# T4 of the value weights added on VectorE from raw buffers on chip; four raw buffers and 67 slots; the stores of x by column, head fetches and the parts of S2 moved

## The chip, the cores and the metric

The kernel runs on one core of one Trainium2 chip. The metric is device time in microseconds (us), lower is better. The engines are named as in the profile: PE is TensorE (PEld its weight loads), DVE VectorE, ACT ScalarE, POOL GpSimd, SP SyncE, which here issues transfers only. POOL issues transfers too, and those that add into their destination all go through it.

## The reference

Two decoder layers over 512 positions of width 2048, in float32. Each layer makes one wide projection of x, splits its columns among three groups of heads, multiplies each group's output by a gate, projects the result and normalises it with the residual.

```python
for l in range(DEPTH):                                  # DEPTH = 2
    h = einsum('bsd,dn->bsn', x, w_in[l])               # 2048 -> 8278 columns
    # 6 heads with a forget bias, 6 heads that see only their 128 best keys (16 index heads
    # score them), 4 heads into 256 memory tokens; each group's output times silu(gate)
    y = concatenate([y_fox, y_dsa, y_mem], axis=-1)
    y = einsum('bsn,nd->bsd', y, w_out[l])
    x = layer_norm(ALPHA * x + y, ln_gain[l], ln_bias[l])
```

## The kernel before

**Products.** Every float32 operand is split into a high part (`whi`, made by ACT) and the rest (`wlo`, made by DVE), and a product is three matmuls: high by high, high by low, low by high (lines 220 to 222). Weights come in chunks of 128 rows by 2048 columns (1 MB, tile `raw`). A chunk is used in two halves of 128 by 1024; each half is split by `split_w` three halves ahead of its matmuls, and `load_w` issues a chunk's load on SP two chunks ahead. There are three `raw` buffers and four `whi`/`wlo` pairs.

**Stages of a layer.** Projection of the memory tokens (`mv`, `mk`), the index heads and their scores (`small`, `iq`, `ix`), memory heads (`mq`, `mg`), **values** (kind `vs`: values, gates and some queries and keys), **heads** (`fq`, `fk`, `dq`, `dk`, each followed by its attention `attend`), and the output projection (`out`). The values and the output use a Strassen-like scheme: seven products, named P1, P7, Q6, Q4, Q5, P2 and Q3, replace eight, and take sums of weight blocks on the right (T1 to T4) and sums of x on the left (S1 to S4).

**The right sides T2 and T4 of the values.** Their chunks are not loaded but "grown". When the P7 chunk has been split, its `raw` buffer is kept, a transfer issued by POOL adds a block of the weights into it, and it becomes Q6's chunk; after Q6 another such transfer adds the (1, 0) block, and it becomes Q4's chunk. `grow_w` (lines 245 to 250) issues them: 32 transfers of 1 MB, 16 for Q6 and 16 for Q4, over two layers and four pairs of column groups. P2's chunk, used between them, is the same (1, 0) block, loaded from the same place in HBM.

**Order.** The program's order is written by hand (a manual schedule): each engine runs its instructions in that order. Side work is written as generators, advanced by `tick`: once in each half chunk, except that attention advances once a chunk while values or output run. `attend` issues, at its start, the fetches of the head's gates and values (`load_head`, line 882, on SP), and two ticks later it begins the transposes. `val_operands` makes S1 to S4 and splits them; `next_x` (line 933) ends a layer: it normalises the residual tiles `z`, transposes them into the next x (`xh`, `xl`), and then stores the 16 `z` tiles to HBM (`x1`, line 956). At the start of the second layer `residual_rows` (line 960) fetches those tiles, applies gain and bias (lines 968 and 969) and stores them again (line 970).

**Slots.** Everything of 128 by 512 float32 lives in one pool of 71 slots (`slot`). A new tile takes a slot that an earlier tile has left, and its first writer waits until the last reader of the earlier tile is done. The pool hands out slots that came free lately, so the distance between the two is often short. SP and POOL issue transfers in order: one that waits for its slot holds all later ones of its engine back.

The lines that the steps below touch: 213 and 214 (`split`), 241 (a chunk's load), 249 (the growing transfer), 466 (first writer of the memory heads' probabilities `pm`), 767 (sums of x), 777, 845 to 863 (values out of PSUM), 882, 968 to 970.

Of the kernel before, what the change touches and what calls it, by code (L numbers as in the profile page):

```python
# [14 lines left out]
ALU = mybir.AluOpType  # L15
AX = mybir.AxisListType

P = 128
# [68 lines left out]
VAL_OPENS = ("P1", "P7", "P2", "Q5")  # L87
VAL_ENDS = ("P1", "Q4", "P2", "Q3")
GROWN = {"Q6": ("P7", (0, 0)), "Q4": ("Q6", (1, 0))}


def layer_chunks(l):
# [80 lines left out]
def kernel(  # L173
# [12 lines left out]
):  # L186
    nc = tc.nc
    consts = ctx.enter_context(tc.tile_pool(name="consts", bufs=1))
    raws = ctx.enter_context(tc.tile_pool(name="raws", bufs=3))
    whl = ctx.enter_context(tc.tile_pool(name="whl", bufs=4))  # L190
    slots = ctx.enter_context(tc.tile_pool(name="slots", bufs=71))
    tiny = ctx.enter_context(tc.tile_pool(name="tiny", bufs=3))
    psum = ctx.enter_context(tc.tile_pool(name="psum", bufs=8, space=bass.MemoryType.PSUM))
    dram = ctx.enter_context(tc.tile_pool(name="dram", bufs=1, space=bass.MemoryType.DRAM))
# [30 lines left out]
    chunks = stream()  # L225
    raw, parts = {}, {}
    sums = {}
    grows = {}
    place = {c[:4]: i for i, c in enumerate(chunks)}
    for i, (kind, l, j, g, (how, key)) in enumerate(chunks):  # L230
        if how == "grown":
            grows[place[kind, l, (key[0], j[1]), g]] = i

    def load_w(i, pieces=1):
        if i < len(chunks) and chunks[i][4][0] != "grown":
# [8 lines left out]

    def grow_w(i):

        if i in grows:
            n = grows[i]
            nc.gpsimd.dma_start(raw[n], wall[chunks[n][4][1][1]], accum_op=ALU.add,
                                max_dma_last_dim=4 * DM)  # L250

    def last_half(i):

# [2 lines left out]
    def split_w(n, pieces=1, between=None):  # L256
        i, h = divmod(n, 2)
        if i < len(chunks):
            if last_half(i) and n < 2 * len(chunks) - 3:
                parts[n] = []  # L260
                for c in range(2):
                    hi, lo = slot("wh", F32R), slot("wl", F32R)
                    split(raw[i][:, h * 1024 + c * 512:h * 1024 + (c + 1) * 512], hi, lo)
                    parts[n].append((hi, lo))
                return
            hi = whl.tile([P, DM // 2], F32R, tag="whi", name=uid("whi"))
            lo = whl.tile([P, DM // 2], F32R, tag="wlo", name=uid("wlo"))
            w = DM // 2 // pieces
            for c in range(pieces):
                r = slice(c * w, (c + 1) * w)  # L270
                split(raw[i][:, h * 1024 + c * w:h * 1024 + (c + 1) * w], hi[:, r], lo[:, r])
                if between and c == 0:
                    between()
            parts[n] = (hi, lo)
            if last_half(i):
                parts[n] = [(hi[:, c:c + 512], lo[:, c:c + 512]) for c in (0, 512)]
            if h:
                t = raw.pop(i)
                if i in grows:
                    raw[grows[i]] = t  # L280


    mem_raw = {}
# [355 lines left out]
    def attend(l, kind, h):  # L639
# [15 lines left out]
        for qb in (3, 1, 0, 2):  # L655
            b, off, w = PACK[qb]
            c = slice(off, off + w)
# [12 lines left out]
                                     scale=rec[:, qb:qb + 1])  # L670

        before.append(probabilities)
        n = HEADS.index(key)
        load_head(("g", key), GATES + n // 4, n % 4)
        load_head(("v", key), VALUES + n // 4, n % 4)
        yield 2
        tp = [bank("pt") for _ in range(3)]
        for kt in range(4):
            tb, toff = PT_PACK[kt]
# [99 lines left out]
    def val_operands():  # L779
        add, sub = ALU.add, ALU.subtract  # L780
        a11, a12, a21, a22 = (0, 0), (0, 1), (1, 0), (1, 1)

        for i in range(4):
            val_sum("S3", i, ((a11, 0, add), (a21, 0, sub), (a11, 1, add), (a21, 1, sub)))
            yield 1
        for i in range(4):
            val_hi("S3", i)
            val_sum("S2", i, (("S3", 0, add), (a22, 0, add), (a22, 1, add)))
            yield 1
            val_lo("S3", i)  # L790
            yield 1
        for i in range(4):
            hi, lo = vleft["S2", i] = slot("vxh", F32R), slot("vxl", F32R)
            nc.scalar.activation(hi, vx["S2", i], AF.Copy, scale=-1.0)
            yield 1
            nc.vector.scalar_tensor_tensor(lo, vx["S2", i], -1.0, hi.bitcast(F32),
                                           op0=ALU.mult, op1=ALU.subtract)
        yield from wait_for("P7")
        making.append("S1")
        for n in range(9):  # L800
            if n < 4:
                val_sum("S1", n, ((a11, 0, add), ("S2", 0, sub), (a11, 1, add)))
            elif n < 8:
                val_sum("S4", n - 4, ((a12, 0, add), ("S2", 0, sub), (a12, 1, add)),
                        vx.pop(("S2", n - 4)))
            yield 1
            if n == 4:
                yield from wait_for("Q6")
            if n:
                name, i = (("S1", n - 1), ("S4", n - 5))[n > 4]  # L810
                val_lo(name, i)
            if n < 8:
                val_hi(*(("S1", n), ("S4", n - 4))[n > 3])
            yield 1
        making.clear()
# [95 lines left out]
    def norm_stats(st):  # L911
        mv, rs = small("mv", 2, bufs=4), small("rs", 1, bufs=4)
        nc.vector.bn_aggr(mv, stats.pop(st).rearrange("p (a b) -> p a b", a=8))
        nc.vector.tensor_scalar(rs, mv[:, 1:2], LN_EPS, None, op0=ALU.add)
        nc.gpsimd.tensor_tensor(rs, rs, mhalf, op=ALU.pow)
        return mv, rs
# [15 lines left out]

    def next_x():

        ms = [norm_stats(st) for st in range(4)]
        for c in range(4):
            for st in range(4):
                normalise(st, c, *ms[st])
            yield 1
        for k in range(KT):  # L940
            c, o = divmod(k, 4)
            tp = bank("xt")
            for st in range(4):
                nc.tensor.transpose(tp[:, st * P:(st + 1) * P], z[st, c][:, o * P:(o + 1) * P], ident)
            xf, hi, lo = slot("xf"), slot("xh", F32R), slot("xl", F32R)
            nc.scalar.activation(xf, tp, AF.Identity, bias=gcol[:, 1, k:k + 1],
                                 scale=gcol[:, 0, k:k + 1])
            nc.scalar.activation(hi, xf, AF.Copy)
            eng = nc.gpsimd if k % 2 else nc.vector
            eng.tensor_tensor(lo, xf, hi.bitcast(F32), op=ALU.subtract)  # L950
            xT[k] = (hi, lo)
            if k % 2:
                yield 1
        for c in range(4):
            for st in range(4):
                nc.gpsimd.dma_start(x1_d[st * P:(st + 1) * P, c * 512:(c + 1) * 512], z.pop((st, c)))
                if st % 2:
                    yield 1

    def residual_rows(l):  # L960

# [89 lines left out]
    for i, (kind, l, j, col, _) in enumerate(chunks):  # L1051
# [28 lines left out]
        for h in range(2):  # L1080
# [9 lines left out]
            if n < 6:  # L1090
                split_mem(n + 2)
            split_w(n + 3)
            for k in range(2 * n - 20, 2 * n - 18) if n < 16 else range(12, 16) if n == 16 else ():
                if k >= 0:
                    split_x(k)
# [264 lines left out]
```

## Time and profile before

| | us |
|---|---|
| median of three runs (1919.09 to 1919.70) | 1919.21 |
| the profiled execution | 1918.99 |
| its span, first to last instruction | 1916.8 |
| PE busy / idle in the span | 1900.9 / 15.9 |
| DVE busy | 1389.3 |
| ACT busy | 969.6 |
| POOL busy | 355.8 |

The granted TensorE clock was 0.998 of full speed. 2.2 us lie around the span. A matmul's busy time in the profile overlaps that of the next one (0.39 us long, one every 0.227 us for 512 columns), so busy time says that PE never waited, not that it could not be fed faster. Layer 0's values run from about 235 to 540 us, its heads to about 805 us and its output to 960 us; the second layer repeats them about 951 us later.

### The profile page before, as it was taken

The page shows a single profiled execution, that of the slowest core. Times are in us where ns is not written, and L with a number is a line of the kernel's source. Part 1 is how long each engine was busy: PE and PEld are TensorE (multiplying, and loading weights), DVE is VectorE, ACT ScalarE, POOL GpSimd, SP SyncE. Part 2 cuts the span into 40 slices and gives each one's busy share as a digit, 9 for nine tenths or more (in the row PEclk, how much of TensorE's full clock was granted, in tenths as well). Part 3 has the DMA queues.
Part 4 walks back from the last instruction along what each step waited for, and adds up shares of the span by engine and source line. Part 5 has one row for each costly group of instructions (what it writes and reads, how often), then busy time and mean ns, then how long its engine had stood idle before and what let it go on. Part 6 is the DMA issues. An engine that isn't in the chain of part 4 may idle for free.

```text
span 1916.8 us, 25327 instructions
## 1 busy us (share of the span) xinstructions
PE 1900.9 (99%) x9282; PEld 1620.7 (85%) x9282; DVE 1389.3 (72%) x2343; ACT 969.6 (51%) x1538; POOL 355.8 (19%) x615
## 2 busy tenths in 40 slices
PE   9999999999999999999999999999999999999997
PEld 8998888888888888888899988888888888888886
DVE  6666657779665677688776777667786666677898
ACT  5565454445444455555475644544454444555552
POOL 0231101111123012110052212111111321112101
PEclk9999999999999999999999999999999999999999
DMA  9699888888988778898778989988889888789856
GB/s 365 230 296 323 213 194 235 241 234 239 263 257 233 245 236 240 250 333 310 247 234 269 283 272 258 238 220 236 244 244 261 261 227 244 240 234 268 342 197 154
DMA packets 110712, 484.57 MB, mean 253 GB/s; under 512 B 11504, under 2 KB 44272, under 8 KB 69500
## 3 DMA queue, kind: packets, MB, share of 16 engines
q0 software_dynamic: 32864, 216.05, 45.6%
q1 hardware_dynamic: 77724, 266.90, 38.8%
q8 instruction: 73, 1.20, 0.3%
q14 instruction: 51, 0.42, 0.1%
HBM read 445.14 MB, written 174.09 MB: 323 GB/s over the span
## 4 chain that ended last, share of the span: by engine, by line
PE 93%; DVE 4%; ACT 2%; issue 1%; DMA 0%; SPq 0%; POOL 0%; DVEq 0%; ACTq 0%; POOLq 0%
PE c L220 12%; PE c L222 12%; PE c L221 12%; PE v L222 11%; PE v L220 11%; PE v L221 11%; PE z L221 4%; PE z L222 4%; PE z L220 4%; PE pt L682 1%; PE ix L600 1%; PE ix L599 1%; PE po L222 1%; PE po L221 1%; PE po L220 1%
## 5 line engine op out<-in xcount | busy, mean ns | idle before, releaser
L214 DVE TENSOR_TENSOR wlo<-raw,whi 128x1024 fp32r<-128x1024 f32 (+1 forms) x497 | 607.0, 1225 | 283.5 <-ACT whi L213 281.3
L213 ACT ACTIVATE whi<-raw 128x1024 fp32r<-128x1024 f32 (+1 forms) x497 | 521.9, 1054 | 381.5 <-PE v L222 243.1
L220 PE MATMUL c<-xh,whi 128*128 128x512 f32 (+1 forms) x1056 | 402.1, 381 | 0.0
L222 PE MATMUL c<-xh,wlo 128*128 128x512 f32 (+1 forms) x1056 | 398.3, 377 | 0.0
L221 PE MATMUL c<-xl,whi 128*128 128x512 f32 (+1 forms) x1056 | 397.3, 376 | 0.0
L222 PEld LDWEIGHTS c<-xh,wlo 128*128 128x128 f32 x1056 | 198.2, 188 | 32.4
L221 PEld LDWEIGHTS c<-xl,whi 128*128 128x128 f32 x1056 | 198.5, 188 | 30.5
L220 PEld LDWEIGHTS c<-xh,whi 128*128 128x128 f32 x1056 | 198.3, 188 | 30.0
L220 PE MATMUL v<-whi,vxh 128*128 128x512 f32 x512 | 199.8, 390 | 0.0
L222 PE MATMUL v<-whi,vxl 128*128 128x512 f32 x512 | 199.3, 389 | 0.0
L221 PE MATMUL v<-wlo,vxh 128*128 128x512 f32 x512 | 199.2, 389 | 0.0
L349 POOL TENSOR_TENSOR seen<-mark,mhalf 128x1 f32<-128x1 f32 x128 | 35.3, 276 | 762.2 <-DVE mark L348 727.3
L221 PE MATMUL z<-wlo,yh 128*128 128x512 f32 (+1 forms) x434 | 168.1, 387 | 2.5 <-DVE wlo L214 2.5
L220 PE MATMUL z<-whi,yh 128*128 128x512 f32 (+1 forms) x434 | 168.4, 388 | 0.0
L222 PE MATMUL z<-whi,yl 128*128 128x512 f32 (+1 forms) x434 | 167.8, 387 | 0.0
L220 PE MATMUL v<-whi,xh 128*128 128x512 f32 x384 | 149.4, 389 | 0.0
L221 PE MATMUL v<-wlo,xh 128*128 128x512 f32 x384 | 149.4, 389 | 0.0
L222 PE MATMUL v<-whi,xl 128*128 128x512 f32 x384 | 149.4, 389 | 0.0
L222 PEld LDWEIGHTS v<-whi,vxl 128*128 128x128 f32 x512 | 96.1, 188 | 20.0
L221 PEld LDWEIGHTS v<-wlo,vxh 128*128 128x128 f32 x512 | 96.1, 188 | 19.9
L220 PEld LDWEIGHTS v<-whi,vxh 128*128 128x128 f32 x512 | 96.1, 188 | 19.6
L221 PEld LDWEIGHTS z<-wlo,yh 128*128 128x128 f32 x434 | 81.5, 188 | 20.0 <-DVE wlo L214 4.2
(220 smaller groups left out, 3031.0 us busy)
## 6 DMA issues: line engine op xcount, KB each, us to landing
raw<-in_wall_dram SPq DMA_DIRECT2D x151, 1024.0 KB, 7.2
sum<-in_wall_dram POOLq DMA_DIRECT2D x64, 1024.0 KB, 11.5
raw<-sum SPq DMA_DIRECT2D x64, 1024.0 KB, 7.1
raw<-in_wall_dram POOLq DMA_DIRECT2D x32, 1024.0 KB, 8.1
v<-vraw POOLq DMA_DIRECT2D x96, 256.0 KB, 4.2
vraw<-v SPq DMA_DIRECT2D x64, 256.0 KB, 6.9
x<-z POOLq DMA_DIRECT2D x32, 256.0 KB, 8.1
memraw<-in_memt_dram SPq DMA_DIRECT2D x16, 256.0 KB, 7.3
```

The lines of the kernel that those rows point to most:

```text
L213: nc.scalar.activation(hi, src, AF.Copy)
L214: nc.vector.tensor_tensor(lo, src, hi.bitcast(F32), op=ALU.subtract)
L220: nc.tensor.matmul(ps, ah, bh, start=start, stop=False, skip_group_check=more)
L221: nc.tensor.matmul(ps, ah, bl, start=False, stop=False, skip_group_check=more)
L222: nc.tensor.matmul(ps, al, bh, start=False, stop=stop, skip_group_check=more)
L349: nc.gpsimd.tensor_tensor(seen, mark, mhalf, op=ALU.mult)
L599: nc.tensor.matmul(o, st[:, qb * P:(qb + 1) * P], kh2[:, :w], start=True, stop=False)
L600: nc.tensor.matmul(o, st[:, qb * P:(qb + 1) * P], kl2[:, :w], start=False, stop=True)
L682: nc.tensor.transpose(tp[tb][:, toff + (qb - kt) * P:toff + (qb - kt + 1) * P], pr[b][:, off + kt * P:off + (kt + 1) * P], ident)
```

## The change

T4 of the values no longer comes from a transfer. P2's `raw` buffer is kept after its split (`lends`, `kept_raw`), and DVE adds it to the buffer that Q6 leaves, in two halves, five halves ahead of Q4's matmuls (`add_w`): 32 additions of 128 by 1024 in place of 16 transfers of 1 MB. For this there is a fourth `raw` buffer (8 KB in each partition), paid for with four of the 71 slots (2 KB each). Three things are moved: `attend` fetches a head's gates and values one tick later; the split of S2 begins six ticks later; and `next_x` stores a column of `z` tiles while it transposes the next one.

```diff
+ADD_STEPS = 5
-    raws = ctx.enter_context(tc.tile_pool(name="raws", bufs=3))
+    raws = ctx.enter_context(tc.tile_pool(name="raws", bufs=4))
-    slots = ctx.enter_context(tc.tile_pool(name="slots", bufs=71))
+    slots = ctx.enter_context(tc.tile_pool(name="slots", bufs=67))
...
-    grows = {}
+    grows, lends, kept_raw = {}, {}, {}
         if how == "grown":
             grows[place[kind, l, (key[0], j[1]), g]] = i
+            if j[0] == "Q4":
+                lends[place[kind, l, ("P2", j[1]), g]] = i
+    lent = {i: n for n, i in lends.items()}
...
     def grow_w(i):
-        if i in grows:
+        if i in grows and grows[i] not in lent:
...
+    def add_w(n):
+        i, h = divmod(n + ADD_STEPS, 2)
+        if i in lent:
+            r = slice(h * 1024, (h + 1) * 1024)
+            nc.vector.tensor_tensor(raw[i][:, r], raw[i][:, r], kept_raw[lent[i]][:, r], op=ALU.add)
+            if h:
+                del kept_raw[lent[i]]
...
                 if i in grows:
                     raw[grows[i]] = t
+                if i in lends:
+                    kept_raw[i] = t
...
         before.append(probabilities)
+        yield 1
         n = HEADS.index(key)
         load_head(("g", key), GATES + n // 4, n % 4)
         load_head(("v", key), VALUES + n // 4, n % 4)
-        yield 2
+        yield 1
...
             val_lo("S3", i)
             yield 1
+        yield 6
         for i in range(4):
             hi, lo = vleft["S2", i] = slot("vxh", F32R), slot("vxl", F32R)
...
     def next_x():
+        def store(st, c):
+            nc.gpsimd.dma_start(x1_d[st * P:(st + 1) * P, c * 512:(c + 1) * 512], z.pop((st, c)))
...
             if k % 2:
+                for st in (o - 1, o) if c else ():
+                    store(st, c - 1)
                 yield 1
-        for c in range(4):
-            for st in range(4):
-                nc.gpsimd.dma_start(x1_d[st * P:(st + 1) * P, c * 512:(c + 1) * 512], z.pop((st, c)))
-                if st % 2:
-                    yield 1
+        for st in range(4):
+            store(st, 3)
+            if st % 2:
+                yield 1
...
             split_w(n + 3)
+            add_w(n)
```

PE's instructions keep their order. Three places on other engines matter below.

DVE, in the values of layer 0, last of the four pairs, while the sums of x for S1 and S4 (`vx`) are made; `wlo` are the splits of weight halves, `vxl` those of the sums. Before:

```order
L214 TENSOR_TENSOR wlo_4112<-raw_4089,whi_4111 128x1024
L767 TENSOR_TENSOR vx_4127<-xh_515,vx_2531 128x256
L767 TENSOR_TENSOR vx_4127<-vx_4127,xl_516 128x256
L767 TENSOR_TENSOR vx_4127<-xh_519,vx_2531 128x256
L767 TENSOR_TENSOR vx_4127<-vx_4127,xl_520 128x256
L214 TENSOR_TENSOR wlo_4134<-raw_4089,whi_4133 128x1024
L777 TENSOR_TENSOR vxl_4109<-vx_4083,vxh_4108 128x512
L214 TENSOR_TENSOR wlo_4154<-raw_3881,whi_4153 128x1024
L852 SCALAR_TENSOR_TENSOR vraw_4169<-v_3961,vraw_3954 128x512
```

The same place in the change:

```order
L215 TENSOR_TENSOR wlo_4117<-raw_4094,whi_4116 128x1024
L261 TENSOR_TENSOR raw_3887<-raw_3887,raw_3970 128x1024
L783 TENSOR_TENSOR vx_4133<-xh_515,vx_2531 128x256
L783 TENSOR_TENSOR vx_4133<-vx_4133,xl_516 128x256
L783 TENSOR_TENSOR vx_4133<-xh_519,vx_2531 128x256
L783 TENSOR_TENSOR vx_4133<-vx_4133,xl_520 128x256
L215 TENSOR_TENSOR wlo_4139<-raw_4094,whi_4138 128x1024
L261 TENSOR_TENSOR raw_3887<-raw_3887,raw_3970 128x1024
L793 TENSOR_TENSOR vxl_4114<-vx_4089,vxh_4113 128x512
L215 TENSOR_TENSOR wlo_4160<-raw_3887,whi_4159 128x1024
L261 TENSOR_TENSOR raw_3926<-raw_3926,raw_4094 128x1024
L869 SCALAR_TENSOR_TENSOR vraw_4176<-v_3967,vraw_3960 128x512
```

One addition now stands behind each of four successive splits (the fourth follows a few rows on, with the next split); nothing else has moved here.

SP, in the heads of layer 0: two fetches of a head's gates and values (`vraw`) and the load of a weight chunk behind them, with the semaphores that each waits for (DMAHW and DMASW are transfers). Before:

```order
L882 DMA vraw_6858<-v_166 128x4x128 [waits DMASW5_49,DMAHW0_49,PE_49,Activation_49]
L882 DMA vraw_6860<-v_163 128x4x128 [waits DMAHW1_49,PE_49]
L241 DMA raw_6965<-in_wall_dram 128x2048 [waits DMAHW2_49,DVE_49]
L882 DMA vraw_7051<-v_166 128x4x128 [waits DMAHW3_49,DVE_49,PE_49]
L882 DMA vraw_7053<-v_163 128x4x128 [waits DMAHW4_49,PE_49]
```

The same in the change:

```order
L899 DMA vraw_6959<-v_166 128x4x128 [waits DMASW7_49,DMAHW0_49,DMASW0_49,PE_49]
L899 DMA vraw_6961<-v_163 128x4x128 [waits DMAHW1_49,DVE_49,PE_49]
L245 DMA raw_6973<-in_wall_dram 128x2048 [waits DMAHW2_49]
L899 DMA vraw_7120<-v_166 128x4x128 [waits DMAHW3_49,DVE_49,PE_49]
L899 DMA vraw_7122<-v_163 128x4x128 [waits DMAHW4_49,DMAHW0_49,PE_49]
```

The chunk's load no longer waits for a DVE split. The two fetches still wait for PE, but for other matmuls. Before, they took slots that the transposes of the probabilities (line 682) had left; in the change, slots that the product of probabilities and values of the head before (`po`) leaves, which comes later.

ACT, in the second layer's memory heads, the last of the four: the probabilities `pm`, a split of S3 (`vxh`) and the splits of two weight halves. Before:

```order
L466 ACTIVATE pm_11429,sums_11427<-sm_11412,nm_11426 128x256 [waits DMASW4_49,DMAHW6_49,DVE_49,PE_49]
L466 ACTIVATE pm_11429,sums_11427<-sm_11412,nm_11426 128x256
L466 ACTIVATE pm_11430,sums_11427<-sm_11413,nm_11426 128x256 [waits PE_49,Activation_49]
L466 ACTIVATE pm_11430,sums_11427<-sm_11413,nm_11426 128x256
L772 ACTIVATE vxh_11441<-vx_11014 128x512 [waits Activation_49]
L213 ACTIVATE whi_11453<-raw_11334 128x1024
```

The same in the change:

```order
L481 ACTIVATE pm_11437,sums_11435<-sm_11420,nm_11434 128x256 [waits DMASW7_49,DVE_49,PE_49]
L481 ACTIVATE pm_11437,sums_11435<-sm_11420,nm_11434 128x256
L481 ACTIVATE pm_11438,sums_11435<-sm_11421,nm_11434 128x256 [waits PE_49,Activation_49]
L481 ACTIVATE pm_11438,sums_11435<-sm_11421,nm_11434 128x256
L788 ACTIVATE vxh_11449<-vx_11022 128x512
L214 ACTIVATE whi_11461<-raw_11342 128x1024
```

The order is the same, but the first row waits for another store of line 970: before, for the one issued at 1177.6 us; in the change, for the one that the trace of before shows issued at 1190.2 us, because the first `pm` tile has taken that store's slot.

## Prediction

> **What bounds the kernel now.** I read the page first: busy times, then the chain that ended last, then what PE waited for.
>
> ```profile
> PE   1900.9 (99%) x9282; PEld 1620.7 (85%) x9282; DVE 1389.3 (72%) x2343; ACT 969.6 (51%) x1538; POOL 355.8 (19%) x615
> ...
> PE 93%; DVE 4%; ACT 2%; issue 1%; DMA 0%; SPq 0%; POOL 0%; DVEq 0%; ACTq 0%; POOLq 0%
> ...
> PE z L221 <- DVE wlo L214: 2.5, 4, 0.7
> PE warm L319 <- POOL mhalf L321: 1.4, 1, 1.4
> PE v L220 <- ACT memh L213: 0.6, 1, 0.6
> PE v L221 <- DVE wlo L214: 0.2, 1, 0.2
> PE v L220 <- ACT whi L213: 0.2, 1, 0.2
> ```
>
> PE is busy for 1900.9 of 1916.8 us, and all the waits that the profile can name sum to 4.9 us, at the start and in the output stage. In the values, where the transfers go, PE waits for nothing. Faster feeding has at most 4.9 us to win anywhere, and about nothing where the change puts it. What the change can do is make PE wait. So I look for places where work is just in time: how late may DVE, ACT or a transfer become before PE stops?
>
> **The additions.** The table of stretches shows a middle part of the values (325 to 365 us) and their last pair in layer 0 (447 to 479 us) and layer 1 (1406 to 1422 us), and the page's group of splits gives the nearest duration. In a row the third pair of numbers is DVE's, the last two are the busy share of the DMA engines and their GB/s.
>
> ```profile
> 325.00:365.00 40.00, 40.00 (x179) 33.10 (x178) 28.31 (x44) 17.01 (x17) 6.09 (x10) 1.00 0.85 251
> ...
> 447.00:455.00 8.00, 8.00 (x37) 6.61 (x36) 6.98 (x12) 3.82 (x4) 1.38 (x3) 1.00 0.99 247
> 455.00:463.00 8.00, 8.00 (x37) 6.64 (x36) 7.86 (x15) 3.17 (x4) 1.92 (x4) 1.00 0.87 320
> 463.00:471.00 8.00, 8.00 (x37) 6.64 (x36) 7.93 (x13) 4.65 (x6) 0.34 (x1) 1.00 0.70 241
> 471.00:479.00 8.00, 8.00 (x37) 6.60 (x37) 7.86 (x14) 4.50 (x6) 0.75 (x2) 1.00 0.67 256
> 1406.00:1414.00 8.00, 8.00 (x37) 6.64 (x36) 7.86 (x15) 2.96 (x4) 2.13 (x4) 1.00 0.93 350
> 1414.00:1422.00 8.00, 8.00 (x37) 6.64 (x36) 7.93 (x12) 4.85 (x6) 0.13 (x1) 1.00 0.68 225
> ...
> L214 DVE TENSOR_TENSOR wlo<-raw,whi 128x1024 fp32r<-128x1024 f32 (+1 forms) x497 | 607.0, 1225 | 283.5 <-ACT whi L213 281.3
> ```
>
> DVE, 72% busy over the span, is full in the last pair from 455 us on (7.86 to 7.93 of 8 us). The addition is not in this trace; its nearest row is the split, also of two 128 by 1024 operands in SBUF: 1.225 us, which I take (bounds: nothing, if DVE always had room, and 1.3 us). All 32 cost 39 us of DVE. In the first three pairs DVE idles more than a quarter of the time (28.31 of 40 us busy), so 24 of the 32 cost nothing; without that cover each would cost up to 1.2 us. The last pair's four fall from 447 to 458 us. From there the timeline of DVE, ACT and PE:
>
> ```profile
> 451.31 1.22 DVE L214 TENSOR_TENSOR wlo<-raw,whi 128x1024 fp32r<-128x1024 f32 x1 [0.88 <-ACT whi L213]
> ...
> 476.59 0.42 DVE L767 TENSOR_TENSOR vx<-vx,xl 128x256 f32<-128x256 f32 x1
> ...
> 481.67 1.23 DVE L214 TENSOR_TENSOR wlo<-raw,whi 128x1024 fp32r<-128x1024 f32 x1 [1.78 <-ACT whi L213]
> ...
> 477.05 0.63 ACT L772 ACTIVATE vxh<-vx 128x512 fp32r<-128x512 f32 x1 [1.28 <-DVE vx L767]
> 477.59 1.05 ACT L213 ACTIVATE whi<-raw 128x1024 fp32r<-128x1024 f32 x1
> 478.73 0.60 ACT L863 ACTIVATE vraw<-v 128x512 f32<-128x512 f32 x1
> ...
> 479.89 0.39 PE L220 MATMUL v<-whi,vxh 128*128 128x512 f32 x1
> ```
>
> Four additions are 4.9 us; DVE's 0.88 us of idle time at 451.31 takes some back, and no further gap follows until 481.67. So DVE runs 4.0 us late from 458 us on. At 476.59 the sum of x that ACT's `vxh` waits for comes 4.0 us late; behind it in ACT's order stand a split and the copy of a PSUM bank (line 863), which ends at 479.33 and frees the bank for the matmul at 479.89. The slack is 0.56 us, so PE stops for 4.0 - 0.56 = 3.4 us. An earlier stop, at a split, is part of the same lateness and adds nothing. Layer 1's rows are the same: **6.8 us** for both layers, with bounds 0 and 2 x 4.9 = 9.8.
>
> **The head fetches.** In the change two fetches of layer 0's heads wait for the last read of the preceding head's `po` product, and the weight load stands behind them on SP. Timeline, and the landing time of that load from its line's view:
>
> ```profile
> 730.58 0.93 SPq L882 DMA_DIRECT2D vraw<-v  x2
> 731.60 0.90 SPq L241 DMA_DIRECT2D raw<-in_wall_dram  x1
> ...
> DMA to landing us min/median/max: 14.1/14.1/14.1
> ...
> 745.77 0.29 PE L222 MATMUL po<-pthl,vl 128*128 128x256 f32 x1
> ...
> 757.90 1.04 ACT L213 ACTIVATE whi<-raw 128x1024 fp32r<-128x1024 f32 x1
> 764.67 0.62 ACT L213 ACTIVATE vh<-vraw 128x512 fp32r<-128x512 f32 x1
> ...
> 766.54 0.39 PE L220 MATMUL po<-pth,vh 128*128 128x512 f32 x1
> ...
> raw<-in_wall_dram SPq DMA_DIRECT2D x151, 1024.0 KB, 7.2
> ```
>
> The fetch can start at 746.1 us, the load at 746.7, and with its own 14.1 us it lands at 760.8: 2.9 us after ACT wanted it (757.90). Queued behind it on ACT are the attention's rows up to `vh`, which ends at 765.29 for a matmul at 766.54, a slack of 1.25. So PE stops for 1.7 us. Layer 1 has such places too, with a load of 15.6 us. I count one stop in each layer: **3.4 us**; bounds 0 (with the median of 7.2 us the load lands at 753.9, in time) and 7 (both such places in both layers).
>
> [...]
>
> **The slot of `pm`.** In layer 1's memory heads ACT's `pm` now waits for the store of line 970 issued at 1190.17 us.
>
> ```profile
> 1190.17 0.60 POOL L970 DMA_DIRECT2D x<-z  x1 [1.72 <-DVE z L969]
> ...
> DMA to landing us min/median/max: 9.0/11.7/17.2
> ...
> 1201.51 0.47 ACT L466 ACTIVATE pm<-sm,nm 128x256 f32<-128x256 f32 x1 [3.17 <-DVE nm L463]
> 1203.85 2.01 ACT L213 ACTIVATE whi<-raw 128x1024 fp32r<-128x1024 f32 x2
> ...
> 1207.42 0.69 DVE L777 TENSOR_TENSOR vxl<-vx,vxh 128x512 fp32r<-128x512 f32 x1 [1.25 <-DMA x<-z]
> 1208.52 0.39 PE L220 MATMUL v<-whi,xh 128*128 128x512 f32 x1
> ```
>
> The five stores of that stretch land in 9.0 to 17.2 us; this one takes 17.2, for a wait on DVE ends with it at 1207.4. ACT would start `pm` there, 5.9 us late. Behind it stand the other three `pm`, `vxh` and the weight split at 1203.85, whose first half ends at 1204.9 for the matmul at 1208.52: PE stops for 2.2 us, and 1.1 more for the `wlo` that follows (1.22 us on DVE). **3.3 us**, bounds 0 (the store lands in 13.9 us or less) and 5.9. The row of the store itself decides for 3.3.
>
> **The rest costs nothing.** The 16 removed transfers were not waited for by PE, and POOL's issues are off the path. The earlier stores of x lie on POOL under the transposes of x on PE, and the first fetch of x comes after all of them. For S2 the tightest pair is the last of its parts and the matmul that reads it first:
>
> ```profile
> 267.84 0.68 DVE L796 SCALAR_TENSOR_TENSOR vxl<-vx,vxh 128x512 fp32r<-128x512 f32 x1
> ...
> 287.22 0.39 PE L222 MATMUL v<-whi,vxl 128*128 128x512 f32 x1
> ```
>
> The parts move by six half chunks of 12 matmuls at 0.227 us, 16.3 us, and 18.7 us lie between, so 2.4 us are left. I take 0; if DVE is late there too, up to 2 us a layer.
>
> **Sum.** 6.8 + 3.4 + 3.3 = 13.5 us on the profiled execution's 1918.99 (span 1916.8 and 2.2 around it, 0.2 below the median of the runs): **1932.5 us**.
>
> **Rivals.**
> - *Only DVE.* The loads and the store land sooner in the new arrangement, and only the additions count: 1918.99 + 6.8 = 1925.8. For it: both other terms hang on single landings of 14 and 17 us.
> - *All places stop.* Each load behind a waiting fetch keeps its long landing, the store lands as late as here and ACT's lateness is paid in full, and S2's parts are late in one layer: 6.8 + 7 + 5.9 + 2 = 21.7, so 1940.7.
> - *The additions find room.* If ACT and PE were not as tight as the 0.56 us says, or DVE ran the addition in half the time, and the landings shortened, 1919 to 1922. Against it: three full windows.
> - *Faster: matmuls run quicker with fewer transfers.* The groups below, each with two more of its size, are 2688 matmuls; 2 ns off each would give 5.4 us, 1913.6; it decides from 1.4 ns. Against it: at DMA shares of 0.99 and 0.67 the windows above hold 37 matmuls each.
>
> ```profile
> L220 PE MATMUL v<-whi,vxh 128*128 128x512 f32 x512 | 199.8, 390 | 0.0
> ...
> L220 PE MATMUL v<-whi,xh 128*128 128x512 f32 x384 | 149.4, 389 | 0.0
> ```
>
> [...]
>
> **How the numbers follow.** Forecast (1929 to 1937) 0.46; only DVE 0.21; all places 0.17; additions find room 0.11; faster 0.05. Less than 0.2%, 3.8 us, cannot be told from no change by a measurement of this kernel. The range takes in the first three, from 1922 to 1941, and leaves out most of the last two and the far end of the third. Slower by over 0.2%: 0.84; within: 0.10; faster: 0.06.
>
> **What would show it.** Right: PE idle of about 3 us near 467 and 480, and again near 1418 and 1431, ended by `wlo` of DVE and the copy of line 863 (now 880) on ACT; a stop at a `po` in the heads ended by `vh` or `vl`; one near the last `ptm` of layer 1. Wrong: no idle time of PE in the last pair of the values although DVE is full there; additions far from 1.2 us; or fetches that wait for nothing.

## The result and the profile after

| kernel | runs | median, us | lowest to highest |
|---|---|---|---|
| before | 4 | 1919.15 | 1918.42 to 1919.70 |
| after | 4 | 1939.11 | 1937.22 to 1940.34 |

The change makes the kernel slower: 1.0103 times the time of before, 95% interval 1.0086 to 1.0121. The forecast was 1932.5 us with a range of 1922 to 1941. The profiled execution spans 1937.4 us where that of before spans 1916.8, so 20.6 us are to be found.

The busy times on the page of after:

```profile
PE 1908.3 (99%) x9282; PEld 1624.3 (84%) x9282; DVE 1425.8 (74%) x2375; ACT 969.4 (50%) x1538; POOL 340.3 (18%) x599
```

DVE has 32 instructions and 36.5 us more, POOL 16 transfers less. PE is busy for 7.4 us more with the same 9282 matmuls, and idle for 29.1 us of its span where it was idle for 15.9. Most of the loss is waiting, so the next view is what PE waited for (total us, times, longest):

```profile
PE z L222 <- DVE wlo L215: 6.6, 4, 3.3
PE v L221 <- ACT whi L214: 4.6, 1, 4.6
PE v L221 <- ACT vraw L880: 3.7, 2, 1.9
PE v L222 <- DVE wlo L215: 1.7, 4, 0.5
```

The waits of before summed to 4.9 us. I then compared the start of every matmul in both traces. The lateness grows at seven stops and nowhere between them, except for a few matmuls right behind three of the stops:

| place in after, us | what it is | stop | slow matmuls behind it |
|---|---|---|---|
| 467 and 482 | last pair of the values, layer 0 | 0.7 + 2.2 | 1.7 |
| 822 | start of the output stage, layer 0 | 1.5 | 0 |
| 1219 | memory heads, layer 1 | 4.9 + 1.0 | 2.0 |
| 1432 and 1447 | last pair of the values, layer 1 | 0.8 + 2.2 | 0 |
| 1787 | start of the output stage, layer 1 | 2.8 | 1.5 |

They sum to 21.3 us; 0.4 us is won at the start, and small differences make up the rest. The first, third and fourth rows are two of the predicted places. No stop stands in the heads. The second and fifth rows, and the column of slow matmuls, were not predicted.

**The last pair of the values**, in the table of stretches (PE, PEld, DVE, ACT and POOL busy, granted clock, DMA share, GB/s), then in the timeline of DVE, ACT and PE at the second stop of layer 0:

```profile
455.00:463.00 8.00, 8.00 (x37) 6.62 (x36) 7.86 (x13) 2.65 (x3) 2.22 (x4) 1.00 0.70 257
463.00:471.00 8.00, 7.49 (x33) 5.88 (x32) 7.86 (x14) 3.44 (x5) 1.08 (x2) 1.00 0.95 354
471.00:479.00 8.00, 8.00 (x37) 6.62 (x36) 7.90 (x14) 4.15 (x5) 1.08 (x2) 1.00 0.72 252
```

```profile
479.76 0.42 DVE L783 TENSOR_TENSOR vx<-vx,xl 128x256 f32<-128x256 f32 x1
...
480.22 0.63 ACT L788 ACTIVATE vxh<-vx 128x512 fp32r<-128x512 f32 x1 [1.93 <-DVE vx L783]
480.75 1.04 ACT L214 ACTIVATE whi<-raw 128x1024 fp32r<-128x1024 f32 x1
...
481.70 1.07 ACT L880 ACTIVATE vraw<-v 128x512 f32<-128x512 f32 x2
...
482.33 0.50 PE L221 MATMUL v<-whi,vxh 128*128 128x512 f32 x1 [1.86 <-ACT vraw L880]
```

DVE was full before and is full after; it only runs later. The sum of x that ended at 477.0 now ends at 480.2. ACT's `vxh` waits for it (1.93 us), the split and the copy of the PSUM bank stand behind `vxh`, and PE waits for the copy. That is the predicted chain, row by row.

**The memory heads of layer 1**, in the view of the store line for the one store issued at 1195.9, and in the timeline:

```profile
L991 POOL DMA_DIRECT2D x<-z x1: 597/597/597, 1195.9 to 1195.9; - x1
...
  ACT pm L481: 11.4, 1
...
DMA to landing us min/median/max: 19.5/19.5/19.5
```

```profile
1215.58 0.47 ACT L481 ACTIVATE pm<-sm,nm 128x256 f32<-128x256 f32 x1 [11.43 <-DMA x<-z]
...
1219.02 0.79 PE L221 MATMUL v<-whi,xh 128*128 128x512 f32 x1 [4.59 <-ACT whi L214]
```

ACT sat idle for 11.43 us until a store had landed whose slot `pm` was given. The store took 19.5 us, where the forecast used the 17.2 us of before.

**The start of the output stage.** DVE's first operations on the residual tiles `z` (line 1011) wait for their loads, and the weight split that PE needs stands behind them. Line 1011 among the groups of after, then the landing of the four first `z` loads (issued 802.0 to 803.7 us) in after, and of the same four in before:

```profile
L1011 DVE SCALAR_TENSOR_TENSOR z<-z,z 128x512 f32<-128x512 f32 x32 | 20.5, 681 | 3.7 <-DMA z<-x 2.5 <-DMA z<-in_x_dram 1.2
```

```profile
L926 POOL DMA_DIRECT2D z<-in_x_dram x4: 810/824/865, 802.0 to 803.7; - x4
...
  DVE z L1011: 1.2, 2
...
DMA to landing us min/median/max: 14.3/16.3/16.9
```

```profile
L909 POOL DMA_DIRECT2D z<-in_x_dram x4: 543/556/604, 799.2 to 800.9; - x4
...
DMA to landing us min/median/max: 9.8/10.3/10.5
```

The loads take 6 us longer, and DVE, which the view of before does not list among those that waited for them, now waits for two.

**The slow matmuls.** The table of stretches at the stop of 482 us, and at the one of 1447 us, which is the same stop in layer 1:

```profile
480.40:482.30 1.90, 0.07 (x1) 0.00 (x0) 1.90 (x3) 1.90 (x4) 0.00 (x0) 1.00 0.33 138
482.30:484.00 1.70, 1.67 (x7) 1.39 (x8) 1.01 (x2) 1.41 (x2) 1.43 (x2) 0.96 0.92 284
484.00:487.50 3.50, 3.50 (x11) 2.68 (x10) 1.58 (x2) 0.85 (x1) 0.37 (x1) 0.53 1.02 248
487.50:491.00 3.50, 3.50 (x17) 2.92 (x16) 1.41 (x2) 1.27 (x2) 0.00 (x0) 1.00 1.05 350
...
1447.60:1450.00 2.40, 2.40 (x11) 1.98 (x12) 1.71 (x2) 1.36 (x2) 1.80 (x2) 1.00 0.88 304
1450.00:1454.00 4.00, 4.00 (x19) 3.34 (x18) 2.05 (x3) 1.70 (x2) 0.00 (x0) 1.00 1.06 216
```

From 484 to 487.5 us the granted clock is 0.53 and eight to nine matmuls run at 0.43 us instead of 0.227. After 1447 us nothing of the kind happens. PE counts as fully busy in both, so neither busy time nor waits show this loss: only the column of the clock and the number of matmuls do.

### The profile page after: what moved, and what is told of

Same layout as the page of the kernel before. It is cut to its first block, busy times and chain, and to the rows that moved or that the text cites. A ratio compares the mean times of both kernels' runs of the same rounds, so it can differ in the third digit from the quotient of the medians.

```text
span 1937.4 us, 25358 instructions
## 1 busy us (share of the span) xinstructions
PE 1908.3 (99%) x9282; PEld 1624.3 (84%) x9282; DVE 1425.8 (74%) x2375; ACT 969.4 (50%) x1538; POOL 340.3 (18%) x599
## 5 line engine op out<-in xcount | busy, mean ns | idle before, releaser
L214 ACT ACTIVATE whi<-raw 128x1024 fp32r<-128x1024 f32 (+1 forms) x497 | 521.3, 1054 | 369.4 <-PE v L223 214.7
L222 PEld LDWEIGHTS v<-wlo,vxh 128*128 128x128 f32 x512 | 96.5, 189 | 19.8
```

The source lines that it names most:

```text
L214: nc.scalar.activation(hi, src, AF.Copy)
L222: nc.tensor.matmul(ps, ah, bl, start=False, stop=False, skip_group_check=more)
```

## Taking the change apart

The first question was which part of the change owns which stop. With before and after at its ends, the runs below form a ladder.

| kernel | median, us | ratio to before, 95% | step, us |
|---|---|---|---|
| before | 1919 | | |
| only the moved code (3 buffers, 71 slots, no additions) | 1919.55 | 1.0003, 0.9994 to 1.0013 | within 0.2% |
| + 67 slots | 1925.92 | 1.0037, 1.0023 to 1.0050 | +6.4 |
| + fourth buffer | 1933.03 | 1.0068, 1.0053 to 1.0083 | +7.1 |
| + 24 additions, first three pairs | 1932.97 | 1.0070, 1.0053 to 1.0087 | -0.1 |
| + 8 additions, last pair: after | 1939.11 | 1.0103, 1.0086 to 1.0121 | +6.1 |

Each ratio is known to 2 or 3 us either way, and a step is the difference of two such kernels. Which stop belongs to which step is therefore read from the traces, and the steps give the size of the costs to a few us only.

**No additions.** The edit to after, in the planner of the additions:

```diff
-            if j[0] == "Q4":
+            if j[0] == "Q4" and False:
```

> The changed kernel with T4 of the values grown by a transfer again, as before the change: the 32 additions are off DVE, the 16 transfers are back; four raw buffers, 67 slots and all moved code stay. Theory: the additions of the last pair alone make the two pairs of stops that the changed kernel shows near 467 and 482 us and near 1432 and 1447 us (2.87 + 2.99 us), and the slow matmuls behind the one at 482 (1.7 us), so 1939.1 - 7.6 = 1931.5 us, with no stop of PE in the last pair of the values. Rival 1: the stops there come from the fourth buffer or the slots: time stays at 1939. Rival 2: the 16 transfers that are back cost about as much elsewhere: no stop in the last pair, yet 1936 or more.

Measured 1933.03 us. The four stops of the last pair are gone from the trace, and the 16 transfers that are back stop PE nowhere. The first theory holds: the additions cost 6.1 us. That is less than the 7.6 us read from one trace; the four runs of this kernel lie between 1928.2 and 1935.0 us, so the two do not contradict each other.

**T4 by a transfer in the last pair alone.**

```diff
-            if j[0] == "Q4":
+            if j[0] == "Q4" and j[1] < PAIRS - 1:
```

> The changed kernel with T4 grown by a transfer in the last of the four pairs alone (8 additions less, 4 transfers more); the other 24 additions stay on DVE. Theory: additions cost nothing where DVE idles a quarter of the time, so the time is that of the kernel with no additions, about 1931.5 us. Rival: every addition costs its share (32 share 7.6 us, 24 of them 5.7), so about 1937.2 us.

Measured 1932.97 us, the same as with no additions: 24 additions of 1.2 us cost nothing that can be measured, 8 cost all of it, and the rival's 1937.2 us lies above all four runs (1930.97 to 1933.68). This is the forecast's cover (DVE idle for a quarter of the time in the first three pairs) tested directly.

**The slots and the fourth buffer.** No additions, and three buffers with 67 slots; then three buffers with 71 slots:

```diff
-    raws = ctx.enter_context(tc.tile_pool(name="raws", bufs=4))
+    raws = ctx.enter_context(tc.tile_pool(name="raws", bufs=3))
```

> The changed kernel with T4 grown by a transfer again and with three raw buffers, still 67 slots and all moved code. Against the kernel with no additions (1933.0 us), which stops PE at the start of the output stage for 0.8 us near 818 and 1.5 us near 1780 with some 1.4 us of slow matmuls behind. Theory: the fourth raw buffer is the cause there, because it lets a load of summed weights start before the z loads; with three buffers that load starts with them and the stops shrink to those of the kernel before: 1933.0 - 3.7 = 1929.3 us. Rival: the 67 slots are the cause (z gets its slots later): 1933. The stop near 1217 us (5.9 us and slow matmuls) belongs to the slots in both and stays.

> The changed kernel with T4 grown by a transfer again, three raw buffers and 71 slots: only the moved code is left of the change (x stored column by column, head fetches and the parts of S2 later). Theory: the moves cost nothing, 1919.2 us, without the stops near 467, 482, 822, 1219, 1432, 1447 and 1787 us. Rival: a part of the 20 us belongs to the moves: 1923 or more, with one of those stops left.

Measured 1925.92 and 1919.55 us. What PE waited for, first with 67 slots, then with 71:

```profile
PE v L221 <- ACT whi L214: 3.6, 1, 3.6
PE z L222 <- DVE wlo L215: 2.7, 5, 0.6
```

```profile
PE z L222 <- DVE wlo L215: 3.2, 5, 0.7
PE warm L334 <- POOL mhalf L336: 1.3, 1, 1.3
PE v L223 <- DVE vxl L813: 1.0, 1, 1.0
```

With 71 slots only small waits are left, and the moves cost nothing that can be told from zero. (The last row is S2's part, the tight pair of the forecast: 1.0 us late in one layer.) With 67 slots there is one stop more, of ACT's split in the memory heads: 3.6 us, 1.0 for the `wlo` behind it, and 1.8 of slow matmuls, which is the measured 6.4 us. With three buffers the output stage has no stop at all beyond those of before, so that one belongs to the fourth buffer. The landing of the four `z` loads with four buffers and no additions, then with three, shows how:

```profile
DMA to landing us min/median/max: 12.4/14.1/15.1
```

```profile
DMA to landing us min/median/max: 11.0/11.2/11.3
```

With four buffers SP issues a load of 1 MB of summed weights at 788.9 us, before the `z` loads; with three it goes out with them, at 799.4:

```profile
L245 SPq DMA_DIRECT2D raw<-sum x1: 847/847/847, 788.9 to 788.9; - x1
```

```profile
799.42 0.33 SPq L245 DMA_DIRECT2D raw<-sum  x1
```

That the buffer is the cause, the two runs show. That it acts through this earlier load is read from the two traces; no run moves the load alone.

The fourth buffer also makes the store of the memory heads land later (18.6 us with three buffers, 20.8 with four), and the stop there longer (3.6 against 5.9 us). Of its 7.1 us, the traces place 3.8 in the output stage, with some 1.4 of slow matmuls among it, and 2.4 in the memory heads; about 1 us is not assigned.

## Trying to remove the stops one by one

**The memory heads.** In after with one edit to `residual_rows`, the stores that hold the slots are issued earlier:

```diff
                 nc.sync.dma_start(t[n], x1_d[st * P:(st + 1) * P, c * 512:(c + 1) * 512])
-            yield 2
+            yield 1
```

> The changed kernel with one edit: the second layer's rows of x are made and stored at every step of the order, not at every second, so that their 16 stores are issued early and no probability tile of the memory heads takes a slot that one of them still reads. Theory: the stop of 4.9 + 1.0 us near 1219 us and the 2.0 us of slow matmuls behind it go, 1939.1 - 7.9 = 1931.2 us. Rival 1: ACT's weight split there is late for another reason (its load lands late): the stop stays, 1939. Rival 2: the closer stores crowd the loads at the start of layer 1 and a new stop takes its place: 1935 or more, with a stop near 1170 to 1200 us.

Measured 1938.80 us: no gain, though the stop at 1219 is gone. The timeline shows where it went:

```profile
1081.63 0.69 DVE L989 TENSOR_TENSOR z<-z,row 128x512 f32<-128x512 f32 x1 [1.80 <-DMA z<-x]
```

DVE waits for a fetch of the rows, and other work of the index stage stands behind it. That is a part of it only: 1.5 us are lost at 1061, before this wait. PE loses 10.5 us against before between 1054 and 1097 us, where after loses none (its waits on ACT's `rel` of line 619 and DVE's `rope` of line 523 are new, and slow matmuls follow). Rival 2 was right that a new stop takes the old one's place, at an earlier place than it named; whether the closer stores crowd that fetch, as it says, is not shown.

Hurrying only the last six of the 16 rows, on the kernel whose last pair has no additions:

```diff
-            yield 2
+            yield 2 if n < 10 else 1
```

> The kernel with T4 of the last pair grown by a transfer (1933.0 us), and the second layer's rows of x made at every second step of the order for the first ten of 16 tiles and at every step only for the last six, so that the last memory head's probability tiles take no slot of a store while the index stage keeps its pace. Theory: making all rows at every step gave back what it won because DVE and ACT were late in the index stage (1054 to 1097 us); with only the last six hurried, those stops stay away and the stop of 5.7 + 1.0 us near 1217 us with its 1.8 us of slow matmuls goes: 1933.0 - 8.5 = 1924.5 us. Rival 1: six hurried tiles are enough to make DVE late in the index stage: a new stop near 1080 to 1110 us, 1930 or more. Rival 2: another tile of the memory heads, which takes a slot of an earlier store, becomes the wait: the stop near 1217 stays or moves to the third head, 1930 or more.

Measured 1922.61 us, ratio 1.0018 (1.0008 to 1.0027). The theory said 1924.5. No stop is left in the memory heads or the index stage, and what PE waits for beyond the waits of before is this group alone, in the output stage, with 1.4 us of slow matmuls:

```profile
PE z L222 <- DVE wlo L215: 6.1, 4, 2.5
```

With the same 67 slots the last head's `pm` no longer waits for a store. So the slots' cost is not a price of having 67 of them, but of how late the store lands whose slot a tile is given.

**The output stage.** Three kernels try to bring the first `z` loads in earlier. In after, the loads of the first two row blocks on SP; in after, the first four on ACT:

```diff
-        nc.gpsimd.dma_start(z[st, dc], src[st * P:(st + 1) * P, dc * 512:(dc + 1) * 512])
+        eng = nc.sync if st < 2 else nc.gpsimd              # first kernel
+        eng = nc.scalar if st < 2 and dc < 2 else nc.gpsimd # second kernel
+        eng.dma_start(z[st, dc], src[st * P:(st + 1) * P, dc * 512:(dc + 1) * 512])
```

> The changed kernel with one edit: the residual loads of the first two row blocks for the output stage (z) are issued by SP, ahead of the weight loads in its queue, instead of by POOL. Theory: with four raw buffers the two loads of summed weights are issued earlier (793 and 804 us, not 800 and 808) and share the DMA engines with the z loads, which land 14 to 17 us after issue instead of 10; behind z in SP's order they cannot, so the stops of 1.5 us near 822 and 2.8 us near 1787 go and the 1.5 us of slow matmuls with them: 1939.1 - 5.8 = 1933.3 us. Rival 1: the z loads land as late as before (what else moves then crowds them, not the weight loads): 1939. Rival 2: the weight loads, now behind z, come too late, and PE waits for a split of ACT at the start of the output stage instead: 1939 or more.

> The changed kernel with one edit: the first four residual loads of the output stage (z) are issued by ACT, not by POOL. In POOL's queue they stand behind the growing of a sum until 802 us, although what they need is free at 787 us; on ACT they start there, 14 us sooner, ahead of the two loads of summed weights. Theory: the z loads' late landing is what holds DVE and then PE, so the stops of 1.5 us near 822 and 2.8 us near 1787 go with the 1.5 us of slow matmuls: 1939.1 - 5.8 = 1933.3 us. Rival 1: the later ones of the eight z loads decide, which stay on POOL: 1937 to 1939. Rival 2: ACT, which spends some 2 to 4 us on issuing, is late with the weight splits, or the last heads' loads land late: a new stop near 790 to 800 us, 1939 or more.

Measured 1950.17 and 1951.69 us, both much slower. On SP, four `z` loads of the second layer hold the queue for 22.7 us, the weight loads behind them go out from 1780.1 us on (the first of them at 1756.6 in after), and PE waits 12.4 us for a split of ACT. This is rival 2. On ACT my premise was false: ACT comes to the four issues at 798.9 us, not at 787, because other work of its order stands before them, and at the end of it ACT waits 4.0 us for DVE's `rope` (line 513). Then they land late as well. SP's queue at 1757 us in the first kernel; the landing of the four in the second:

```profile
1757.27 22.70 SPq L927 DMA_DIRECT2D z<-x  x4
```

```profile
L927 ACTq DMA_DIRECT2D z<-in_x_dram x4: 383/540/653, 798.9 to 800.5; - x4
...
DMA to landing us min/median/max: 11.8/21.8/25.3
```

The third kernel starts from the one at 1922.6 us and issues the four loads on POOL, but one step of the order earlier, ahead of the transfer at which POOL stood; beside it the same edit to the kernel before:

```diff
-                for st, dc in RES_LOADS.get(step, ()):
+                for st, dc in RES_LOADS.get(step, ()) if step else ():
                     load_res(l, st, dc)
...
+        if kind != "out" and i + 1 < len(chunks) and chunks[i + 1][0] == "out":
+            for st, dc in RES_LOADS[0]:
+                load_res(l, st, dc)
         tick(kind)
```

> The kernel with T4 of the last pair grown by a transfer and the last six rows of x hurried (1922.6 us), with the first four residual loads of the output stage issued one step of the order earlier, ahead of the growing of a sum at which POOL's queue stands until 797 us (and until 1751 us in the second layer). What they need is free at 782 us, so they start near 788 us, some 9 us sooner. Theory: the late landing of these four loads is what is left of the loss: the stops of 1.8 us near 819 and 1.9 us near 1772 and the 1.4 us of slow matmuls behind go, and with them the waits of the output stage that the kernel before has too (2.5 us): 1922.6 - 5.1 = 1917.5 us, with 1916 to 1918 slightly faster than the kernel before. Rival 1: the loads start sooner but land late all the same, in the crowd of weights and sums: 1922. Rival 2: they crowd the head's fetches and weights near 790 to 800 us and a new stop takes their place: 1922 or more.

> The kernel before with nothing changed but the first four residual loads of the output stage, issued one step of the order earlier as in the run beside it. Theory: its four waits of PE in the output stage (2.5 us, each for a split of DVE that stands behind the residual) go in part: 1916.7 to 1918. It tells whether a gain of the run beside it belongs to the change or to the earlier loads alone. Rival: those waits are ended by DVE's own load, not by the loads: 1919.

Measured 1926.37 us (1.0040, 1.0026 to 1.0054) and 1919.35 us (1.0001, 0.9992 to 1.0009). The `z` loads are issued at 789.1 and land in 12.0 to 13.3 us, 11 to 13 us sooner than in the kernel that this one starts from. But the load of weights issued 0.3 us behind the first of them, on SP, now takes 30.5 us, where that kernel shows 19.8; that row, and what PE then waits for:

```profile
DMA to landing us min/median/max: 30.5/30.5/30.5
```

```profile
PE z L222 <- DVE wlo L215: 4.0, 6, 0.8
PE z L221 <- ACT whi L214: 3.0, 2, 2.6
```

The stop has passed from DVE's residual to ACT's weight split, in the second layer with slow matmuls behind it. In these 20 us the DMA engines are full (share 1.03 to 1.04 from 790 to 820 us in after and in the kernel without additions; 0.94 and 0.98 in before until 810), and here the loads that went first made another late. In the kernel before the same loads came early without harm and without gain: its waits there are ended by DVE's own work. No version faster than before was found.

**The head fetches.** In after, the two fetches at their former place:

```diff
         before.append(probabilities)
-        yield 1
         n = HEADS.index(key)
         load_head(("g", key), GATES + n // 4, n % 4)
         load_head(("v", key), VALUES + n // 4, n % 4)
-        yield 1
+        yield 2
```

> The changed kernel with the two head fetches at their former place in the code, one step of the order earlier (x stored column by column, S2's parts, additions, buffers and slots as changed). Theory: the later fetches cost nothing, because the weight load behind them on SP now lands in about 8 us and not 14, ahead of ACT's need: 1939.1 us, the same stops. Rival 1: the later place costs what the prediction said, in places that the stops of PE do not show by name: 1936 or less. Rival 2: the later place is what keeps PE from stopping with 67 slots: a stop in the heads, 1941 or more.

Measured 1942.21 us (1.0121, 1.0106 to 1.0136), 3 us more than after, though the intervals overlap. There is no stop in the heads in either kernel. The difference stands at the start of the output stage, at 823 us, where this kernel stops for 2.5 us and not 1.5, and 1.6 us of slow matmuls follow. The theory holds in that the later fetches cost nothing in the heads; that the fetches' place reaches the output stage it did not say, and one profile of each is little to build on.

**Stops made on purpose.** In before, idempotent operations of DVE ahead of one split at six places, to see what follows a stop:

```diff
+            for k, at in enumerate(STOPS):                      # (6, 12, 18, 24, 30, 36)
+                if kind == "vs" and l == 0 and i == vs0 + at and h == 0:
+                    r = slice(1024, 2048)
+                    for _ in range(STOP_OPS[k]):                # (5, 6, 7, 8, 9, 11)
+                        nc.vector.tensor_tensor(raw[i + 1][:, r], raw[i + 1][:, r],
+                                                raw[i + 1][:, r], op=ALU.max)
```

> The kernel before with 5, 6, 7, 8, 9 and 11 extra operations of DVE (a half chunk's maximum with itself, 1.2 us each) put ahead of one weight split at each of six places of the first layer's values, 33 us apart. With the splits three half chunks ahead of PE, PE should stop for about 0, 0, 1.7, 2.9, 4.1 and 6.6 us. Theory: the slow matmuls that the changed kernel shows (0.43 us a matmul and a granted clock near 0.6 for some 3 us) follow from a stop of PE longer than about 2 us, whatever ended it and whatever the transfers do: the granted clock falls after the three longer stops, for some 1.7 us each, and not after the shorter ones: 1919.2 + 15.3 + 5.1 = 1939.6 us. Rival: those slow matmuls come from what else is busy there (transfers, DVE and ACT catching up): no fall of the clock behind these stops, 1934.5 us.

Measured 1962.52 us. I had the lengths wrong, since DVE has other work at these places: PE stops for 0, 2.2, 8.2, 4.9, 7.4 and 10.2 us, and for 2.0 at the copy of line 863 in the last pair, which is late as in after. But the question is answered. The stretches behind the 2.2 us stop and behind the 4.9 us one:

```profile
328.00:332.00 4.00, 4.00 (x19) 3.28 (x18) 3.97 (x7) 3.21 (x5) 0.70 (x1) 1.00 0.63 104
...
408.00:412.00 4.00, 4.00 (x10) 3.13 (x11) 3.96 (x6) 1.29 (x2) 1.45 (x2) 0.50 0.64 100
```

At the same DMA share, with DVE as full, 19 matmuls run after the one stop and 10 after the other. The granted clock falls after all four stops of 4.9 us and more (it is 0.50 to 0.62 from 368 to 370, 408 to 412, 450 to 454 and 495 to 499 us) and after neither of the two of 2.0 to 2.2 us. In this run the theory holds in that the fall follows the stop and not the transfers or DVE, and the rival falls. Where the limit lies this run leaves open: in after a stop of 2.0 us was enough (see the end).

## Why the prediction was right in sign and how it was wrong in its parts

- **The additions** (6.8 us): measured 6.1 us by the runs; the trace of after has 5.9 us of stops there and 1.7 of slow matmuls. The duration taken from the split (1.225 us) was measured as 1.218 us, the row below; the chain was as described. The sum of x came 3.2 us later and not 4.0, and each layer stopped for 2.9 us where 3.4 were forecast. Right. That matmuls run faster with fewer transfers, the fourth rival, did not happen: the stretches of 455 and 471 us still hold 37 of them in 8 us.

```profile
L261 DVE TENSOR_TENSOR raw<-raw,raw 128x1024 f32<-128x1024 f32 x32 | 39.0, 1218 | 0.0
```

- **The head fetches** (3.4 us): nothing. The wait came true: the fetch went out at 749.39 us, behind a `po`, and the load at 750.70. The step that failed is "with its own 14.1 us it lands at 760.8". It landed in 8.0 us, at 758.7, and ACT's split took it up at 762.1. The load of 15.6 us in layer 1 went out at 1652.5 us and landed in 7.7. Here stands the view of the load's line at 750 to 751 us:

```profile
L245 SPq DMA_DIRECT2D raw<-in_wall_dram x1: 1096/1096/1096, 750.7 to 750.7; - x1
...
DMA to landing us min/median/max: 8.0/8.0/8.0
```

  The 14.1 us were no property of that load: the same load takes 12.9 us with only the moved code and 18.1 us in after with the fetches at their former place. Which of the transfers around it makes the difference is not shown. That the load would keep its 14.1 us behind two fetches was my estimate, and no run shows it: it stood behind two fetches, those of 749.39 us, and took 8.0.
- **The slot of `pm`** (3.3 us): the mechanism was right, the size was too small. The step is "this one takes 17.2": with 67 slots alone the store takes 18.6 us, 1.4 more, which with 1.8 us of slow matmuls turns the 3.3 us into the 6.4 us measured; in after the store takes 19.5 us, the stop is 5.9 us and 2.0 us follow. This stop took over the lengthening of the landing it hung on.
- **"The rest costs nothing"** failed for the fourth buffer, which the sum did not price at all: 7.1 us. It was seen as room for P2's chunk. It also let SP issue a load of summed weights 10.5 us earlier (788.9 and not 799.4 us), at the crowded start of the output.
- **No term for the clock.** 5.2 of the 20.6 us are matmuls at half clock behind three stops.

13.5 us were forecast and 20.0 measured: 3.4 too much in the heads, some 10 too little in the other two places and the clock. The two errors have opposite signs, so part of the agreement is luck. The time, above the 1929 to 1937 us of the forecast itself, lies in the range because the range took in the case in which all places stop, not because that case came: no head stopped.

## What to carry to other kernels

One more buffer was not only room: here it let a load start 10.5 us earlier (788.9 and not 799.4 us) in a stage that the change does not aim at, and where the DMA engines were full (share 1.03) other transfers paid (the four `z` loads landed in 14.1 us and not 11.2, the median). Look, before adding it, at every wait that is just in time there. Work moved to an engine was free where that engine idled and cost most of its length where it was full (8 additions of 1.22 us, 6.1 us); the same addition did both, so the choice can be made stretch by stretch. A transfer's time from issue to landing was no constant of the transfer: one weight load of the heads took 14.1, 12.9, 8.0 and 18.1 us in four kernels. Carry such a time into a forecast as a range, not as a number.

## What the runs showed of the hardware

A short stop of PE cost more than its length at three places of after: 1.7, 2.0 and 1.5 us of slow matmuls follow. In the traces of after and of all the experiments I counted the stops of 1 us and more behind the first 60 us; a stop's length is here the interval between two matmul starts less the usual 0.227 us, so the two of the output stage in after count as 2.3 and 3.5 us. Of 8 stops under 2.0 us none was followed by slow matmuls; of 16 between 2.0 and 2.7 us four were; of 20 from 3.1 to 14 us all were. The loss was some 1 to 2.7 us, for long stops as for short ones, and the fall began 2.5 to 5.1 us after the stop's start: at 483.9 for the stop that begins at 480.4. The same stop in the two layers of after (2.0 us each) cost 1.7 us more in one and nothing more in the other.

In after this goes with where the stop lies. The granted clock is halved there in three stretches, from 483.87 to 487.28, from 1217.73 to 1224.56 and from 1787.76 to 1791.17 us. They are 3.41, 6.83 and 3.41 us long, and their beginnings lie 215 and 167 times 3.413 us apart. I cut this trace into steps of 3.413 us, counted from these beginnings, and took PE's idle time in each (by the modelled ends of the matmuls). Between 60 and 1920 us five steps at full clock hold more than 1 us of it. The three with 1.86, 2.99 and 3.29 us are followed by half clock; the two with 1.4 and 1.2 us, from 818.4 and 1446.4 us, are not. The table of stretches, cut at the steps, shows it for the two equal stops. The one of layer 0 lies within one step (PE busy for 1.56 of 3.42 us); the one of layer 1 is parted by an edge (2.74 and 2.23 us busy), and the clock stays:

```profile
480.45:483.87 3.42, 1.56 (x8) 1.26 (x8) 2.73 (x4) 3.26 (x5) 1.29 (x2) 1.00 0.55 180
483.87:487.28 3.41, 3.41 (x10) 2.64 (x9) 1.71 (x2) 0.63 (x1) 0.50 (x1) 0.50 1.05 272
1442.98:1446.39 3.41, 2.74 (x13) 1.93 (x11) 3.34 (x6) 1.48 (x3) 0.00 (x0) 1.00 0.91 299
1446.39:1449.81 3.42, 2.23 (x10) 1.84 (x11) 2.73 (x4) 2.57 (x4) 1.80 (x2) 1.00 0.64 211
1449.81:1453.22 3.41, 3.41 (x17) 2.83 (x16) 2.24 (x3) 1.06 (x1) 0.00 (x0) 1.00 1.03 219
```

These are five steps of one trace. What sets the clock they do not show.
